# Mixer A of a hybrid encoder: the second pair of heads takes its chunks in exchanged order, and the low-rank operand is padded to 128 rows

## The chip, the cores and the metric

The kernel is one program on one core of a Trainium2 chip. Its engines are TensorE (PE; its weight loads are listed as PEld), VectorE (DVE), ScalarE (ACT), GpSimd (POOL) and SyncE (SP), which issues DMAs. Each engine works through its own queue in order and waits on semaphores for the others. The metric is the device time of one execution in microseconds (us), less is better; a kernel's time is the median of its runs.

## What is computed

A two-layer encoder over 1024 tokens of width 1024. In each layer the normed input goes through one input product into four mixers A, B, C and D of 256 columns each, through an output product and then through a feed-forward network. Mixer A is the one that is changed: a recurrence over tokens with a 64x64 state per head, four heads.

```python
def _rwkv7_scan(r, w, k, v, kk, b):
    def step(state, inp):
        r_t, w_t, k_t, v_t, kk_t, b_t = inp
        sa = jnp.einsum('bhvk,bhk->bhv', state, -kk_t)
        state = (state * w_t[:, :, None, :]
                 + sa[..., None] * b_t[:, :, None, :]
                 + v_t[..., None] * k_t[:, :, None, :])
        return state, jnp.einsum('bhvk,bhk->bhv', state, r_t)
...
def _rwkv7_mixer(p, mu, w0, w_up, a0, a_up, g_up, k_k, k_a, r_k, ln_g, ln_b):
    p = p + (p_prev - p) * mu
    r, k, v, wd, ad, gd = _split(p, A_SIZES)
    w_log = -jax.nn.softplus(-(w0 + jnp.tanh(wd) @ w_up).astype(f32)) - 0.5
    decay = jnp.exp(-jnp.exp(w_log))
    a = jax.nn.sigmoid((a0 + ad @ a_up).astype(f32))
    g = jax.nn.sigmoid(gd) @ g_up
```

`w_up` and `a_up` have 32 rows, `g_up` has 64: these are the low-rank products.

## The kernel before

The sequence is worked through in two halves of 512 tokens per layer. The large products (input, output and feed-forward products) are written in `product`, `product2` and `pair`: they run on PE with 128 rows and 128 columns of the array, 512 or 256 moving columns, and their results stand in the PSUM tile `pm`. Here they are called the main products. Beside them run the mixers as generators that are stepped by `weave` and `beside`; a scheduler of the language then sets one fixed order per engine from priorities and its own cost model, so that mixer instructions stand between main products in PE's queue.

Mixer A (`mixA`, `piece`) goes over a half in four blocks of 128 tokens, so there are 16 pieces in all. A block is two chunks of 64 tokens (`par` 0 and 1), and its four heads are two pairs (`hp` 0 and 1) of two (`h`). All its products stand in the PSUM tile `pa`, a bank of 128x512. A piece runs these groups of products; PE runs a product in f32 as two records in the trace:

- the low-rank products with the weights `lw`: two single ones for the decay, two for `a`, on 32 rows of the array, and two for the gate on 64 rows; in the trace `pa<-lora,cst`;
- `pa<-RA,KB`: the products of keys and queries inside a chunk pair, eight of 64 rows; their masked results are the tiles `G`;
- the inverse of a triangular matrix per chunk and head in `solve` (VectorE) and `inverse`: a first level of 16x16 blocks (`pa<-DT,G` and `pa<-D,V`, 16 products each on tiles of 32x32) and a second of 32x32 blocks (`pa<-XT,G` and `pa<-D,VT`, four products each per chunk);
- for each chunk, one after the other since the state `M` goes from one into the next: `part` (`pa<-cst,RA` and `pa<-VS,G`, six products, 12 records, whose result lies on 64 partitions, so on half of the array's columns), then a copy to `Us`, then `pa<-Us,Xs` (four products of 64x64), a copy into `VS`, a second `part` for the output `Y`, and `pa<-VS,KBt`, which with the whole array updates the state;
- transposes and the product with `rkH` with the whole array.

In `part` both pairs of heads work on the same chunk, so that all its products of one call use the same 64 columns of the array.

Of the kernel before, what the change touches and what calls it, by code (L numbers as in the profile page):

```python
# [85 lines left out]
class Kern:  # L86
# [133 lines left out]
    def consts(self):  # L220
# [45 lines left out]
        self.plast = self.const([128, L, UA], "plast")  # L266
        self.M = [self.const([128, 128], f"M{hp}") for hp in range(2)]
# [26 lines left out]
    def layer_params(self, l):  # L294
# [5 lines left out]
        self.lw = self.const([128, 256], "lw")  # L300
        nc.sync.dma_start(out=self.lw, in_=a["lora"][l])
# [416 lines left out]
    def shifted(self, l, hf, b, u, n, name):  # L718
# [14 lines left out]
        for i in range(n):  # L733
            self.act(o[:, i, :], t[:, i, 1:], AF.Copy, scale=self.omu[:, u + i:u + i + 1])
            self.stt(o[:, i, :], t[:, i, 0:128], self.pc[l]["mu"][:, u + i:u + i + 1], o[:, i, :], ALU.mult, ALU.add)
        return o

    def piece(self, l, hf, b, lo):
# [9 lines left out]

        Lc = self.sa([128, 2, 128], name="Lc")
        ta = self.sa([128, 2, 128], name="ta")  # L750
        ps = self.misca()
        for hp, cc, ch in hps:
            self.mm(ps[:, ch], self.lw[0:32, ch], lo[0:32, :], True, True, (0, 0))
            self.act(Lc[:, hp, :], ps[:, ch], AF.Tanh, scale=0.5, bias=self.hw0[:, cc])
        ps = self.misca()
        for hp, cc, ch in hps:
            self.mm(ps[:, ch], self.lw[32:64, ch], lo[32:64, :], True, True, (32, 0))
            self.act(ta[:, hp, :], ps[:, ch], AF.Tanh, scale=0.5, bias=self.ha0[:, cc])
# [88 lines left out]

        Y = self.sa([128, 2, 128], name="Y")
        for par in range(2):
            u0, y0 = 64 * (1 - par), 64 * par  # L850
            us, ys = slice(u0, u0 + 64), slice(y0, y0 + 64)
            heads = [(hp, h, slice(64 * h, 64 * h + 64), slice(hp * 128 + h * 64, hp * 128 + h * 64 + 64))
                     for hp in range(2) for h in range(2)]
# [17 lines left out]
            nc.scalar.copy(out=Y[ys], in_=ps[ys, 0:256].rearrange("p (r d) -> p r d", r=2))  # L871
            for hp, cc, ch in hps:
                self.mm(ps[:, 256 + hp * 128:384 + hp * 128], KBt[:, hp * 2 + par, :], VS[:, hp, par, :], True, True)
            mt = self.sa([128, 2, 128], name="mt")
            for hp, cc, ch in hps:
                self.tt(mt[:, hp, :], ps[:, 256 + hp * 128:384 + hp * 128], self.M[hp], ALU.add)
                self.stt(self.M[hp], mt[:, hp, :], WC[:, hp * 2 + par:hp * 2 + par + 1], self.cs["mH"], ALU.mult, ALU.mult)
# [17 lines left out]
        for hp, cc, ch in hps:  # L895
            nc.tensor.transpose(ps[:, ch], Y[:, hp, :], self.ident)
            self.act(yt[:, hp, :], ps[:, ch], AF.Identity, scale=c["rlng"][:, cc], bias=c["rlnb"][:, cc])
        self.tt(yt, yt, v, ALU.add)
        ps = self.misca()
        for hp, cc, ch in hps:  # L900
            self.mm(ps[:, ch], self.lw[64:128, ch], lo[64:128, :], True, True, (64, 0))
# [44 lines left out]
    def inverse(self, G, XB):  # L946
# [24 lines left out]
        for par, o, e in blocks:  # L971
            for ix in range(4):
# [11 lines left out]
        for par in range(2):  # L984
            p0 = 64 * (1 - par)
            a, b = slice(p0, p0 + 32), slice(p0 + 32, p0 + 64)
            for ix in range(4):
                self.mm(ps[b, ix * 32:ix * 32 + 32], G[par][a, ix, p0 + 32:p0 + 64], XT[a, ix * 32:ix * 32 + 32], True, True, (p0, p0 + 32))
            nc.scalar.copy(out=VT[b].rearrange("p i t -> p (i t)"), in_=ps[b, 0:128])
            for ix in range(4):  # L990
                self.mm(ps[a, 128 + ix * 32:160 + ix * 32], VT[b, ix, :], D[b, ix, :], True, True, (p0 + 32, p0))
            nc.scalar.copy(out=Xs[a, :, 32:64], in_=ps[a, 128:256].rearrange("p (i t) -> p i t", i=4))
# [340 lines left out]
NCOL = 6728  # L1333
# [17 lines left out]
WC = 16  # L1351
# [191 lines left out]
```

## Time and profile before

| | us |
|---|---|
| median of 3 runs (lowest, highest) | 3074.94 (3074.18, 3076.03) |
| the profiled execution | 3089.47 |
| its span, first to last instruction | 3087.7 |
| PE busy | 2959.4 |
| PE's weight loads busy | 2487.4 |
| DVE busy | 2068.9 |
| ACT busy | 1372.4 |
| POOL busy | 620.8 |

A row of a timeline gives the start in us from the span's start, the time from the first start to the last end of a run of like instructions, engine, line, operation, output and inputs, the part of the array (rows\*columns), the shape of the input, and the count. Matmuls are pipelined: the next one starts before the end of the one ahead, so what a product costs is read from starts rather than from durations. The granted clock is TensorE's as a share of its full 2.4 GHz.

### The profile page before, as it was taken

The page shows a single profiled execution, that of the slowest core. Times are in us where ns is not written, and L with a number is a line of the kernel's source. Part 1 is how long each engine was busy: PE and PEld are TensorE (multiplying, and loading weights), DVE is VectorE, ACT ScalarE, POOL GpSimd, SP SyncE. Part 2 cuts the span into 40 slices and gives each one's busy share as a digit, 9 for nine tenths or more (in the row PEclk, how much of TensorE's full clock was granted, in tenths as well). Part 3 has the DMA queues.
Part 4 walks back from the last instruction along what each step waited for, and adds up shares of the span by engine and source line. Part 5 has one row for each costly group of instructions (what it writes and reads, how often), then busy time and mean ns, then how long its engine had stood idle before and what let it go on. Part 6 is the DMA issues. An engine that isn't in the chain of part 4 may idle for free.

```text
span 3087.7 us, 49210 instructions
## 1 busy us (share of the span) xinstructions
PE 2959.4 (96%) x17560; PEld 2487.4 (81%) x17560; DVE 2068.9 (67%) x4721; ACT 1372.4 (44%) x2732; POOL 620.8 (20%) x659
## 2 busy tenths in 40 slices
PE   6999998999989999999999999998999999999999
PEld 5887886877778888987888887987778888878887
DVE  4667676689697675668774656567677665555555
ACT  3445443344354444454544433455454445333333
POOL 2016253246451010100111111110111111111111
PEclk8999987889999999999999999999999999999999
DMA  7458555445452424463423224553333332513332
GB/s 258 137 162 276 160 176 155 134 143 166 150 170 74 124 89 147 144 194 97 133 87 111 82 90 152 147 165 115 96 90 104 104 111 65 204 59 101 113 97 75
DMA packets 276596, 405.74 MB, mean 131 GB/s; under 512 B 74496, under 2 KB 148736, under 8 KB 276352
## 3 DMA queue, kind: packets, MB, share of 16 engines
q1 hardware_dynamic: 276352, 402.61, 41.7%
q8 instruction: 139, 2.28, 0.3%
q14 instruction: 105, 0.86, 0.1%
HBM read 343.47 MB, written 59.02 MB: 130 GB/s over the span
## 4 chain that ended last, share of the span: by engine, by line
PE 52%; DVE 2%; ACT 1%; DMA 1%; issue 1%; SPq 1%; POOL 0%; ACTq 0%; DVEq 0%; POOLq 0%
PE pm L186 44%; PE pa L186 3%; PE px L186 2%; PE S L186 1%; PE px L1088 1%; PE pn L186 0%; DMA raw<-pA 0%; ACT hr L494 0%; DVE hr L189 0%; DMA wr<-in_wout 0%; ACT L198 0%; PE px L1030 0%; DMA wr<-in_wint 0%; DMA NB<-G 0%; SPq L915 0%
## 5 line engine op out<-in xcount | busy, mean ns | idle before, releaser
L186 PE MATMUL pm<-hh,hr 128*128 128x512 f32 (+1 forms) x3328 | 1095.9, 403 | 24.4 <-ACT p L198 13.5
L186 PEld LDWEIGHTS pm<-hh,hr 128*128 128x128 f32 (+1 forms) x3328 | 627.4, 190 | 168.5 <-issue 10.9
L494 ACT CAST hr<-wr 128x1024 fp32r<-128x1024 f32 (+2 forms) x496 | 426.6, 862 | 638.5 <-PE pm L186 531.4
L189 DVE TENSOR_TENSOR hr<-wr,hr 128x1024 fp32r<-128x1024 f32 (+2 forms) x496 | 511.6, 1033 | 270.2 <-ACT hr L494 261.6
L186 PE MATMUL pm<-hl,hr 128*128 128x512 f32 (+1 forms) x1664 | 667.7, 401 | 3.1 <-DVE hl L195 3.1
L186 PE MATMUL pm<-mh,hr 128*128 128x512 f32 x1408 | 462.6, 399 | 5.4 <-ACT Lc L198 2.1
L186 PE MATMUL pm<-hr,hh 128*128 128x256 f32 x2048 | 399.9, 293 | 0.0
L186 PEld LDWEIGHTS pm<-hl,hr 128*128 128x128 f32 (+1 forms) x1664 | 316.6, 190 | 71.3 <-DVE hl L195 5.3
L186 PEld LDWEIGHTS pm<-hr,hh 128*128 128x128 f32 x2048 | 327.3, 195 | 7.2 <-issue 0.5
L660 POOL TENSOR_TENSOR y<-y,y 128x512 f32<-128x512 f32 x88 | 117.4, 1334 | 1050.7 <-DVE y L189 376.9
L186 PEld LDWEIGHTS pm<-mh,hr 128*128 128x128 f32 x1408 | 265.8, 189 | 62.0 <-ACT Lc L198 2.3
L195 DVE SCALAR_TENSOR_TENSOR y<-pm,cst,y 128x511 f32<-128x511 f32 x352 | 261.7, 744 | 73.2 <-ACT y L198 69.2
L186 PE MATMUL pm<-hr,hl 128*128 128x256 f32 x1024 | 295.6, 290 | 0.0
L186 PE MATMUL pm<-ml,hr 128*128 128x512 f32 x704 | 276.9, 393 | 0.0
L195 DVE SCALAR_TENSOR_TENSOR x<-pm,cst,x 128x512 f32<-128x512 f32 x224 | 167.1, 747 | 140.2 <-PE pm L186 139.7
L198 ACT ACTIVATE p<-S,cst 128x512 f32<-128x512 f32 (+3 forms) x288 | 165.5, 581 | 104.6 <-DVE cst L189 69.1
L186 PEld LDWEIGHTS pm<-hr,hl 128*128 128x128 f32 x1024 | 199.0, 195 | 1.6 <-issue 0.2
L1066 DVE TENSOR_REDUCE cst<-S 128x1 f32<-128x512 f32 (+3 forms) x288 | 154.0, 549 | 61.4 <-PE S L186 59.8
L186 PEld LDWEIGHTS px<-V,ct 128*128 128x128 f32 x1152 | 154.2, 200 | 30.2 <-ACT ct L1090 21.6
L186 PE MATMUL px<-V,ct 128*128 128x64 f32 x1152 | 157.9, 280 | 17.3 <-ACT ct L1090 15.4
L186 PE MATMUL pm<-yh,hr 128*128 128x512 f32 x512 | 166.1, 398 | 6.6 <-ACT yh L618 5.8
L198 ACT ACTIVATE y<-pm,cst 128x512 f32<-128x512 f32 x176 | 136.9, 778 | 76.4 <-PE pm L186 75.9
(237 smaller groups left out, 4130.6 us busy)
## 6 DMA issues: line engine op xcount, KB each, us to landing
wr<-in_up SPq DMA_DIRECT2D x176, 512.0 KB
ar<-in_ada SPq DMA_DIRECT2D x192, 256.0 KB
wr<-in_wint SPq DMA_DIRECT2D x64, 512.0 KB
wr<-in_down SPq DMA_DIRECT2D x128, 256.0 KB
wr<-in_wout SPq DMA_DIRECT2D x32, 512.0 KB
wr<-in_win SPq DMA_DIRECT2D x28, 512.0 KB
ks<-qkB SPq DMA_DIRECT2D x192, 64.0 KB
wr<-in_down SPq DMA_DIRECT2D x64, 192.0 KB
```

The source lines that it names most:

```text
L186: return self.nc.tensor.matmul(out, lhsT, rhs, start=start, stop=stop, **kw)
L189: self.nc.vector.tensor_tensor(out=out, in0=a, in1=b, op=op)
L195: self.nc.vector.scalar_tensor_tensor(out=out, in0=a, scalar=s, in1=b, op0=op0, op1=op1)
L198: self.nc.scalar.activation(out=out, in_=in_, func=func, **k)
L494: self.nc.scalar.copy(out=h, in_=r)
L660: nc.gpsimd.tensor_tensor(out=ya, in0=ya, in1=yg, op=ALU.mult)
L1066: nc.vector.tensor_reduce(out=nm[:, i:i + 1], in_=S_[:, 0:n], axis=AX.X, op=ALU.max, negate=True)
L1088: nc.tensor.transpose(ps[:, j:j + 128], pc[:, j:j + 128], self.ident)
```

## The change

In every step the second pair of heads (`hp` 1) now takes the other place of the two chunks in its tiles. This is done by exchanging the two groups of 64 tokens of that pair where its operands are read (`swapped`, in `shifted`, in the low-rank products and at the end of `piece`). Step `step` treats chunk `step` of both pairs, but its rows lie on `par = (step, 1 - step)`: on different halves of the 128 partitions, and so of the array's columns.

- `part`, the `Us` products and both levels of `inverse` are written so that products on different tiles of the array alternate; the second level takes both halves in one loop, where it had one loop after the other.
- `Us` and `Y` are copied as 128x128 where they were 64x256. `VS` is copied in two parts, by VectorE and by ScalarE, where VectorE copied both.
- `pa<-RA,KB` is written as 16 products of 64x64 in place of eight of 64x128.
- The low-rank weights are laid out as three matrices of 128 rows, zero outside their own rows, so that the products take all 128 rows of the operand.

```diff
-        self.lw = self.const([128, 256], "lw")
-        nc.sync.dma_start(out=self.lw, in_=a["lora"][l])
+
+        for i, r in enumerate((slice(0, 32), slice(32, 64), slice(64, 128))):
+            nc.sync.dma_start(out=self.lw[r, i, :], in_=a["lora"][l, r, :])
...
+            if i:
+                oi = oi.rearrange("p (c t) -> p c t", c=2)
+                t1, t0_ = self.swapped(t1), self.swapped(t0_)
...
+    def swapped(self, t):
+
+        return t.rearrange("p (c t) -> p c t", c=2)[:, ::-1, :]
...
-            self.mm(ps[:, ch], self.lw[0:32, ch], lo[0:32, :], True, True, (0, 0))
+            self.mm(ps[:, ch], self.lw[:, 0, ch], los[hp], True, True)
...
-                for h in range(2):
-                    hs = slice(64 * h, 64 * h + 64)
-                    self.mm(pss[h][:, i * 128:i * 128 + 128], flat(KB[hs, hp, 2 * par:2 * par + 2, :]),
-                            flat(RA[hs, hp, 2 * par:2 * par + 2, :]), True, True, (64 * h, 0))
+                for cq in range(2):
+                    for h in range(2):
+                        hs = slice(64 * h, 64 * h + 64)
+                        self.mm(pss[h][64 * cq:64 * cq + 64, i * 128:i * 128 + 128], KB[hs, hp, 2 * par + cq, :],
+                                flat(RA[hs, hp, 2 * par:2 * par + 2, :]), True, True, (64 * h, 64 * cq))
...
-            def part(rows, r0, j):
-
-                for hp, cc, ch in hps:
-                    self.mm(ps[rows, ch], RA[:, hp, 2 * par + j, :], self.M[hp], True, False, (0, r0))
-                    for p, h, hs, o in heads:
-                        if p == hp:
-                            self.mm(ps[rows, o], G[par][:, hp * 2 + h, rows], VS[:, hp, par, hs], False, h == 1, (0, r0))
-
-            part(us, u0, 1 - par)
-            Us = self.sa([128, 256], name="Us")
-            nc.scalar.copy(out=Us[us, :], in_=ps[us, 0:256])
-            for hp, h, hs, o in heads:
-                self.mm(ps[us, 256 + o.start:256 + o.stop], Xs[us, hp * 2 + h, :], Us[us, o], True, True, (u0, u0))
-            nc.vector.tensor_copy(VS[us, :, par, :], ps[us, 256:512].rearrange("p (r d) -> p r d", r=2))
-            part(ys, y0, par)
+            def part(rows, r0, c0, j):
+
+                for hp in range(2):
+                    s = par[hp]
+                    self.mm(ps[rows[hp], c0:c0 + 128], RA[:, hp, 2 * s + (1 - s if j else s), :], self.M[hp], True, False, (0, r0[hp]))
+                for h in range(2):
+                    for hp in range(2):
+                        self.mm(ps[rows[hp], c0 + 64 * h:c0 + 64 * h + 64], G[par[hp]][:, hp * 2 + h, rows[hp]],
+                                VS[:, hp, par[hp], 64 * h:64 * h + 64], False, h == 1, (0, r0[hp]))
+
+            part(us, u0, 0, 1)
+            Us = self.sa([128, 128], name="Us")
+            nc.scalar.copy(out=Us, in_=ps[:, 0:128])
+            for h in range(2):
+                for hp in range(2):
+                    self.mm(ps[us[hp], 128 + 64 * h:192 + 64 * h], Xs[us[hp], hp * 2 + h, :], Us[us[hp], 64 * h:64 * h + 64],
+                            True, True, (u0[hp], u0[hp]))
+            nc.vector.tensor_copy(VS[us[0], 0, par[0], :], ps[us[0], 128:256])
+            nc.scalar.copy(out=VS[us[1], 1, par[1], :], in_=ps[us[1], 128:256])
+            part(ys, y0, 256, 0)
...
-        for par, o, e in blocks:
-            for ix in range(4):
+        for ix in range(4):
+            for par, o, e in blocks:
                 self.mm(ps[o:o + 32, ix * 32:ix * 32 + 16], G[par][o:o + 16, ix, o:o + 32], DT[o:o + 16, ix * 32:ix * 32 + 16], True, True, (o, o))
...
-            for ix in range(4):
+        for ix in range(4):
+            for par, p0, a, b in halves:
                 self.mm(ps[b, ix * 32:ix * 32 + 32], G[par][a, ix, p0 + 32:p0 + 64], XT[a, ix * 32:ix * 32 + 32], True, True, (p0, p0 + 32))
```

The scheduler makes a new order for every engine. Three places show what becomes of it. The first is PE at the first call of `part` in the first piece, in the kernel before. `G_2097` is the tile of chunk 0, `VS` and `RA` are operands, `cst` holds the state, `pm` is a main product.

```order
L186 MATMUL pm<-hr,hh 128x256 x2
L186 MATMUL pm<-hr,hl 128x256
L186 MATMUL pa<-cst,RA 64x128
L186 MATMUL pa<-VS,G_2097 64x64 x2
L186 MATMUL pa<-cst,RA 64x128
L186 MATMUL pa<-VS,G_2097 64x64 x2
L186 MATMUL pm<-hr,hh 128x256 x2
```

The same call in the changed kernel, where `G_2100` and `G_2101` are the tiles of chunk places 0 and 1:

```order
L186 MATMUL pm<-hr,hh 128x256
L186 MATMUL pa<-cst,RA 64x128 x2
L186 MATMUL pa<-VS,G_2100 64x64
L186 MATMUL pa<-VS,G_2101 64x64
L186 MATMUL pa<-VS,G_2100 64x64
L186 MATMUL pa<-VS,G_2101 64x64
L186 MATMUL px<-V,ct 128x64
```

The products of one pair stood behind those of the other; now one of each pair follows one of the other.

The second place is PE at the inverse's second level, chunk place 1 of the same piece, in the kernel before (chunk place 0 stands in an earlier burst of its own, with `G_2097`):

```order
L186 MATMUL pm<-hr,hl 128x256
L186 MATMUL pm<-hr,hh 128x256
L186 MATMUL pa<-XT,G_2098 32x32 x4
L186 MATMUL pm<-hr,hh 128x256
L186 MATMUL pm<-hr,hl 128x256
```

and in the changed kernel:

```order
L186 MATMUL pm<-hr,hl 128x256
L186 MATMUL pm<-hr,hh 128x256 x2
L186 MATMUL pa<-XT,G_2100 32x32
L186 MATMUL pa<-XT,G_2101 32x32
L186 MATMUL pa<-XT,G_2100 32x32
L186 MATMUL pa<-XT,G_2101 32x32
L186 MATMUL pa<-XT,G_2100 32x32
L186 MATMUL pa<-XT,G_2101 32x32
L186 MATMUL pa<-XT,G_2100 32x32
L186 MATMUL pa<-XT,G_2101 32x32
L186 MATMUL pm<-hr,hl 128x256
```

Two bursts between main products became one of eight products that alternate.

The third place is ACT at the first state step. In the kernel before the copy of `Us` is followed by other stages' work and then by the copy of `Y`:

```order
L866 COPY Us<-pa 64x256
L546 COPY pt<-pm 128x512
L494 CAST hr<-wr 128x1024
L1090 COPY ct<-px 128x128
L198 ACTIVATE v<-raw,cst 128x128 x2
L198 ACTIVATE yB<-px,cst 128x64
L198 ACTIVATE p,cst<-S,cst 128x256 x2
L871 COPY Y<-pa 64x256
```

In the changed kernel a copy of half of `VS` stands between them, behind other stages' instructions:

```order
L884 COPY Us<-pa 128x128
L198 ACTIVATE yB<-px,cst 128x64
L198 ACTIVATE p,cst<-S,cst 128x256 x2
L549 COPY pt<-pm 128x512
L497 CAST hr<-wr 128x1024
L198 ACTIVATE v<-raw,cst 128x128
L890 COPY VS<-pa 64x128
L198 ACTIVATE v<-raw,cst 128x128
L1117 COPY ct<-px 128x256
L198 ACTIVATE p,cst<-S,cst 128x384 x2
L892 COPY Y<-pa 128x128
```

The second `part` of the step waits for this copy and for VectorE's.

## Rows read from the trace of the kernel before

**Rows 1.** The page's first part: busy time, share of the span, instructions of each engine.

```profile
PE 2959.4 (96%) x17560; PEld 2487.4 (81%) x17560; DVE 2068.9 (67%) x4721; ACT 1372.4 (44%) x2732; POOL 620.8 (20%) x659
```

**Rows 2.** Sums by stretch, PE: stretch, length, busy (records), granted clock, DMA share, GB/s.

```profile
440.00:830.00 390.00, 355.38 (x1988) 0.85 0.50 154
830.00:2650.00 1820.00, 1776.24 (x10592) 0.98 0.38 117
```

**Rows 3.** The same sums for PE's work on mixer A's tile pa alone.

```profile
80.00:440.00 360.00, 60.54 (x658) 0.98 0.58 182
440.00:830.00 390.00, 57.57 (x573) 0.85 0.50 154
830.00:2650.00 1820.00, 195.61 (x2162) 0.98 0.38 117
```

**Rows 4.** Timeline of PE around one call of part.

```profile
205.79 0.40 PE L186 MATMUL pm<-hr,hh 128*128 128x256 f32 x2
206.03 0.28 PE L186 MATMUL pm<-hr,hl 128*128 128x256 f32 x1
206.24 0.43 PE L186 MATMUL pa<-cst,RA 128*64 128x128 f32 x2
206.51 0.40 PE L186 MATMUL pa<-VS,G 128*64 128x64 f32 x4
206.74 0.38 PE L186 MATMUL pa<-cst,RA 128*64 128x128 f32 x2
206.96 0.39 PE L186 MATMUL pa<-VS,G 128*64 128x64 f32 x4
207.28 0.50 PE L186 MATMUL pm<-hr,hh 128*128 128x256 f32 x2
```

**Rows 5.** Timeline of PE around the state update, which has the whole array.

```profile
238.11 0.39 PE L186 MATMUL pm<-hl,hr 128*128 128x512 f32 x1
238.33 0.39 PE L186 MATMUL pm<-hh,hr 128*128 128x512 f32 x1
238.56 0.61 PE L186 MATMUL pa<-VS,KBt 128*128 128x128 f32 x4
238.93 0.48 PE L186 MATMUL pm<-hh,hr 128*128 128x512 f32 x1
```

**Rows 6.** Timeline of PE around one low-rank product.

```profile
106.03 0.28 PE L186 MATMUL pm<-hr,hl 128*128 128x256 f32 x1
106.24 0.48 PE L186 MATMUL pa<-lora,cst 32*128 32x128 f32 x2
106.65 0.50 PE L186 MATMUL pm<-hr,hh 128*128 128x256 f32 x2
```

**Rows 7.** Timeline of PE around one burst of RA-KB.

```profile
199.99 0.28 PE L186 MATMUL pm<-hr,hl 128*128 128x256 f32 x1
200.20 1.16 PE L186 MATMUL pa<-RA,KB 64*128 64x128 f32 x8
201.28 0.50 PE L186 MATMUL pm<-hr,hh 128*128 128x256 f32 x2
```

**Rows 8.** Timeline of PE: products of the modulation, on four column strips in turn.

```profile
31.56 3.64 PE L186 MATMUL pm<-ar,cst 128*32 128x128 f32 x64
```

**Rows 9.** Timeline of PE: one burst of the Us products.

```profile
210.80 0.68 PE L186 MATMUL pa<-Us,Xs 64*64 64x64 f32 x8
```

**Rows 10.** Timeline of PE around one burst of the inverse's second level.

```profile
187.82 0.28 PE L186 MATMUL pm<-hr,hh 128*128 128x256 f32 x1
188.03 0.43 PE L186 MATMUL pa<-XT,G 32*32 32x32 f32 x8
188.39 0.38 PE L186 MATMUL pm<-hr,hh 128*128 128x256 f32 x1
```

**Rows 11.** Timeline of PE: one burst of the inverse's first level.

```profile
170.00 0.88 PE L186 MATMUL pa<-DT,G 16*32 16x16 f32 x32
```

**Rows 12.** Waits of PE: who waited for whom, total us, times, longest.

```profile
PE pa L186 <- DVE VS L869: 2.7, 2, 2.1
```

More of the change, by code (lines that the diff above doesn't have):

```diff
@@ L266, in consts @@
         self.plast = self.const([128, L, UA], "plast")
+        self.lw = self.const([128, 3, 256], "lw")
+        nc.gpsimd.memset(self.lw, 0.0)
         self.M = [self.const([128, 128], f"M{hp}") for hp in range(2)]
@@ L747, in flat @@
             return t.rearrange("p a b -> p (a b)")
+        los = (lo, self.swapped(lo))
         Lc = self.sa([128, 2, 128], name="Lc")
@@ new lines, in piece @@
+        for step in range(2):
+            par = (step, 1 - step)
+            u0 = [64 * (1 - s) for s in par]
+            us = [slice(u, u + 64) for u in u0]
+            y0 = [64 * s for s in par]
+            ys = [slice(y, y + 64) for y in y0]
+            ps = self.misca()
+            def part(rows, r0, c0, j):
[16 more added lines that the diff above has]
+            part(ys, y0, 256, 0)
+            nc.scalar.copy(out=Y[:, step, :], in_=ps[:, 256:384])
@@ L872, in piece @@
             for hp, cc, ch in hps:
-                self.mm(ps[:, 256 + hp * 128:384 + hp * 128], KBt[:, hp * 2 + par, :], VS[:, hp, par, :], True, True)
+                self.mm(ps[:, ch], KBt[:, hp * 2 + par[hp], :], VS[:, hp, par[hp], :], True, True)
             mt = self.sa([128, 2, 128], name="mt")
             for hp, cc, ch in hps:
-                self.tt(mt[:, hp, :], ps[:, 256 + hp * 128:384 + hp * 128], self.M[hp], ALU.add)
-                self.stt(self.M[hp], mt[:, hp, :], WC[:, hp * 2 + par:hp * 2 + par + 1], self.cs["mH"], ALU.mult, ALU.mult)
+                self.tt(mt[:, hp, :], ps[:, ch], self.M[hp], ALU.add)
@@ L878, in piece @@
+                self.stt(self.M[hp], mt[:, hp, :], WC[:, hp * 2 + par[hp]:hp * 2 + par[hp] + 1], self.cs["mH"], ALU.mult, ALU.mult)
             yield
@@ L896, in piece @@
             nc.tensor.transpose(ps[:, ch], Y[:, hp, :], self.ident)
-            self.act(yt[:, hp, :], ps[:, ch], AF.Identity, scale=c["rlng"][:, cc], bias=c["rlnb"][:, cc])
-        self.tt(yt, yt, v, ALU.add)
+        p4 = ps[:, 0:256].rearrange("p (a t) -> p a t", a=4)
+        for hp, cc, ch in hps:
+            self.act(four(yt)[:, hp], p4[:, 1:3, :] if hp else p4[:, 0:4:3, :], AF.Identity, scale=c["rlng"][:, cc], bias=c["rlnb"][:, cc])
+        self.tt(yt[:, 0, :], yt[:, 0, :], v[:, 0, :], ALU.add)
+        self.tt(four(yt)[:, 1], four(yt)[:, 1], self.swapped(v[:, 1, :]), ALU.add)
         ps = self.misca()
         for hp, cc, ch in hps:
-            self.mm(ps[:, ch], self.lw[64:128, ch], lo[64:128, :], True, True, (64, 0))
+            self.mm(ps[:, ch], self.lw[:, 2, ch], lo, True, True)
         self.tt(flat(yt), flat(yt), ps[:, 0:256], ALU.mult)
@@ L966, in inverse @@
         blocks = [(par, 64 * (1 - par) + 32 * e, e) for par in range(2) for e in range(2)]
-        for par, o, e in blocks:
-            for ix in range(4):
+        for ix in range(4):
+            for par, o, e in blocks:
                 self.mm(ps[o:o + 32, ix * 32:ix * 32 + 16], G[par][o:o + 16, ix, o:o + 32], DT[o:o + 16, ix * 32:ix * 32 + 16], True, True, (o, o))
         nc.scalar.copy(out=V[:, :, 0:16], in_=ps[:, 0:128].rearrange("p (i t) -> p i t", i=4)[:, :, 0:16])
-        for par, o, e in blocks:
-            for ix in range(4):
+        for ix in range(4):
+            for par, o, e in blocks:
                 self.mm(ps[o:o + 32, 128 + ix * 16:144 + ix * 16], V[o:o + 32, ix, :], D[o:o + 32, ix, 16:32], True, True, (o, o))
@@ L983, in inverse @@
         ps = self.misca()
[L984 to L987, printed above, removed]
+        halves = [(par, 64 * (1 - par), slice(64 * (1 - par), 64 * (1 - par) + 32), slice(64 * (1 - par) + 32, 64 * (1 - par) + 64))
+                  for par in range(2)]
+        for ix in range(4):
+            for par, p0, a, b in halves:
                 self.mm(ps[b, ix * 32:ix * 32 + 32], G[par][a, ix, p0 + 32:p0 + 64], XT[a, ix * 32:ix * 32 + 32], True, True, (p0, p0 + 32))
+        for par, p0, a, b in halves:
             nc.scalar.copy(out=VT[b].rearrange("p i t -> p (i t)"), in_=ps[b, 0:128])
-            for ix in range(4):
+        for ix in range(4):
+            for par, p0, a, b in halves:
                 self.mm(ps[a, 128 + ix * 32:160 + ix * 32], VT[b, ix, :], D[b, ix, :], True, True, (p0 + 32, p0))
+        for par, p0, a, b in halves:
             nc.scalar.copy(out=Xs[a, :, 32:64], in_=ps[a, 128:256].rearrange("p (i t) -> p i t", i=4))
@@ L1332 @@
 PN, PO = 6000, 1
-NCOL = 6728
+NCOL = 7240
 PX = 5500
```

14 lines of the change are left out of this document (5 added, 9 removed).

## The prediction

> **What bounds the kernel now.** I read the busy shares first: PE is busy 96% of the span [rows 1], so the question is whether that holds where mixer A runs, and what a product of mixer A costs PE. The sums by stretch come next [rows 2]: from 830 to 2650 us PE is busy 1776 of 1820 us at a granted clock of 0.98, and from 440 to 830 us it is busy 355 of 390 at 0.85. So in the long stretch there is little for PE to wait for, and time taken off PE's queue is time off the span; in the short one the clock has been lowered for a part of it and the gaps are larger, so less of a saving arrives. The same sums for mixer A's tile alone [rows 3] tell how its work lies: 60.5 + 195.6 = 256.1 of its 313.7 us (82%) lie in 80 to 440 and 830 to 2650 us, and 57.6 us (18%) in the short stretch. From 2650 us on there is none.
>
> Busy time is not what a burst costs. **How a burst is priced:** between main products PE starts one every 0.12 us (205.79 to 206.03 for two, 256 columns, [rows 4]) or 0.22 us (238.11 to 238.33, 512 columns, [rows 5]). I take the start of the main product behind a burst minus the start of the last one ahead, less one such step, and add what the pair behind lasts longer than usual (in [rows 4] 0.50 instead of 0.40 us for two of 256, in [rows 5] 0.48 instead of 0.39 for one of 512), since the second of the pair starts late.
>
> **The change part by part.** There are 16 pieces (two layers, two halves, four blocks of 128 tokens). A program product in f32 shows as two records.
>
> *The low-rank products* (four single ones per piece for decay and a, one pair for the gate) had 32 or 64 rows of the array, and have all 128 now, padded with zeros. Before, a single one costs 106.65 - 106.03 - 0.12 + 0.10 = 0.60 us [rows 6]. What the same shape costs with the whole array is the KBt burst of four records: 238.93 - 238.33 - 0.22 + 0.09 = 0.47 us, so 0.12 a record and 0.24 for two [rows 5]. The difference is what PE loses in going into and out of a tiled shape: 0.60 - 0.24 = 0.36 us, 64 times, 23.0 us. The gate's pair is four records on 64 rows; the nearest row is the RA-KB burst of eight on 64 rows, 201.28 - 199.99 - 0.12 + 0.10 = 1.27 us [rows 7]; less four records of 0.12 that is 0.79, against 0.47 after, 0.32 us, 16 times, 5.1 us. Together **28.1 us**. The decay's product now waits for all rows of the low-rank operand, a tanh and an affine step more; I take nothing, and as a bound the nearest wait of PE for a VectorE result in this mixer, 1.35 us on the mean [rows 12], at 16 pieces: 22 us.
>
> *The state products* (`part`, 64 bursts). One costs 207.28 - 206.03 - 0.12 + 0.10 = 1.23 us [rows 4]. All twelve records of one lie on the same 64 columns; the six of one pair take 206.96 - 206.51 = 0.45 us. Now the pairs lie on different column halves and alternate. Do halves run side by side? The trace has the answer for column strips: 64 records of 128 columns in a row, each on the next of four strips, take 3.64 us, 0.057 each [rows 8], half or less of the 0.12 of [rows 5]. So the second pair's 0.45 us is hidden behind the first: 64 x 0.45 = **28.8 us**.
>
> *The Us products* (32 bursts of eight records). They alternate now between two diagonal quarters. Eight take 0.68 us [rows 9], the last four of VS-G in [rows 4] 0.39, so four fewer in line are worth 0.29: 32 x 0.29 = **9.3 us**, if quarters overlap.
>
> *The inverse's second level.* Two bursts of eight records became one of sixteen on two tiles, for XT-G and for D-VT alike. One burst costs 188.39 - 187.82 - 0.12 + (0.38 - 0.28) = 0.55 us [rows 10]. With the tiles side by side, sixteen cost what eight do: a burst is saved, 2 x 16 x 0.55 = **17.6 us**. If they ran in line, eight more records would take at most 188.39 - 188.03 = 0.36 us, and 0.19 would be left: 6.1 us, the lower end.
>
> *The inverse's first level.* 32 records on four diagonal tiles take 0.88 us one tile after the other [rows 11]; cycled, each tile has eight, as in [rows 10], 0.43. Saved 0.45 us, for DT-G and for D-V, which has as many: 2 x 16 x 0.45 = **14.4 us**. Lower end nothing.
>
> First the rows on that: in [rows 11] 32 records take 0.88 us where eight on one tile take 0.43, so a further one costs (0.88 - 0.43)/24 = 0.019 us, less than half of 0.36/8 = 0.045 in line; tiles of different rows and columns overlap already where one follows another, though all write one bank. The Trainium skill ("TensorEngine Tiling (Array Packing)", Restrictions and Gotchas, Gotcha 1) says that different row tiles cannot access the same PSUM bank simultaneously. By that rule the two inverse levels and Us would keep their order in line, and the result would be the second rival's; the trace speaks against it.
>
> *RA-KB.* Eight records of 64 rows and 128 columns became sixteen of 64 by 64, alternating halves. Side by side they take the same time: I take zero. In line they would add 8 x (201.28 - 200.20)/8 = 1.08 us to each of 32 bursts, 34.6 us.
>
> *Pieces.* In the new order of PE some bursts are cut by other products that stand in between, RA-KB above all: I count some 15 more fragments than before. Going in and out costs about 0.2 to 0.3 us (0.60 - 0.24 above, less): **minus 4 us**.
>
> *Other engines.* Us and Y are copied as 128x128 rather than 64x256, which is less ACT time. The second half of VS, one copy on DVE, is one on DVE and one on ACT. PE waits for DVE's copy twice in the whole run, 2.7 us in all, 2.1 the longest [rows 12]. Behind it in PE's queue stands `part`, and behind that the main products, all held while it waits. On ACT the copy may queue behind another stage's work. Lower bound zero, upper bound the mean of those two waits at each of 32 steps, 32 x 1.35 = 43 us; I take zero, since ACT's Us copy in the same chain has no entry among PE's waits of that size. One more memset and four more parameter loads are outside every chain: zero.
>
> **Sum.** 28.1 + 28.8 + 9.3 + 17.6 + 14.4 - 4 = 94.2 us of PE's queue. 82% of it, 77 us, comes off in full; of the 17 us in the short stretch I take half, 8.5. That is 86 us: a span of 3087.7 - 86 = 3002. The profiled execution itself took 3089.47 us, 14.5 above the median of the plain runs, 3074.94; I take the saving off the median: **2989 us**.
>
> **The rivals.**
> *Rival 1, the gain returns as waits.* PE's queue shortens, but the chain of a piece (copies on ACT and DVE, two trips through DRAM) doesn't, and the ACT copy of VS is late at most steps. Against: 44 us of idle in 1820. Price: the 43 us above; 3075 - 86 + 43 = 3032.
> *Rival 2, tiles of different rows don't run together.* Then Us gives nothing (-9.3), the second level 6.1 instead of 17.6, the first nothing (-14.4): 94.2 - 35.2 = 59 us, of which 91% (86 of 94) arrive, 54: 3021. Against it, [rows 11]. For it stands the Trainium skill's sentence above.
> *Rival 3, no tiles run together.* Left are 28.1 + 6.1 - 34.6 = about zero: 3075, no change; the alternation does not do what it says. Against: [rows 8].
> *Rival 4, slower.* Each change of tile empties the array, as the entry into a tiled shape does now: 206.24 - 206.03 - 0.12 = 0.09 us. The new orders alternate some 78 times more per piece (20 in `part`, 6 in Us, 14 in the second level, 24 in the first, 14 in RA-KB): 1248 x 0.09 = 112 us on top of rival 3: 3187. With no overlap it decides from 5 ns per alternation. Against: 64 alternations at 0.057 us with the product included.
> *Rival 5, more.* The short stretch gains in full too, and shorter bursts of small products there let the clock stay up: another 17 us and more; 2968.
>
> **How the numbers follow.** Forecast 0.60 (about 2972 to 3010), rival 1 0.17, rival 2 0.07, rival 3 0.04, rival 4 or another slowdown 0.06, rival 5 0.06. The range runs from rival 5 to beyond rival 1: 2963 to 3038, leaving out rivals 3 and 4 and the tails. A measurement of this kernel tells 0.2% (6 us) from no change. Faster is everything but rivals 3 and 4: 0.90; same 0.04; slower 0.06.
>
> **What would show it.** Right: single low-rank products at 0.24 us with no longer main product behind; `part` at about 0.78 us; sixteen XT-G records within about 0.45; RA-KB still about 1.25. Wrong: alternating records spaced as before (rival 3) or wider (rival 4); PE's waits for VS on ACT over 20 us (rival 1).

## The result and the profile after

The changed kernel takes 3024.1 us, median of 4 runs (3017.75 to 3029.51), beside 3075.49 for the kernel before (4 runs). The ratio is 0.9831, with an interval of 0.9816 to 0.9846: 47 to 57 us less, 51 at the median. The forecast was 2989 with a range of 2963 to 3038, so the sign and the range held, and the saving was 51 us where 86 had been expected. The time lies outside the band of 2972 to 3010 that the prediction gave its main case, and close to the 3032 of its rival 1.

The profiled execution took 3017.75 us. The page's first part, which answers to [rows 1]:

```profile
PE 2871.6 (95%) x17816; PEld 2419.6 (80%) x17816; DVE 2073.8 (69%) x4737; ACT 1361.4 (45%) x2760; POOL 609.2 (20%) x660
```

PE's busy time fell by 87.8 us. Its idle time rose: 3087.7 - 2959.4 = 128.3 us before, 3016.0 - 2871.6 = 144.4 us after. So PE was relieved of about as much as forecast, and a part of that came back as idle time. (The two profiled executions lie 14 us above and 6 us below the medians of their kernels, so what is read from them can be off by that much.)

The bursts, from PE's timeline after (start, us, engine, line, operation, array, shape, count). In order: a low-rank product, RA-KB, the inverse's second level, Us, `part`, the inverse's first level.

```profile
99.53 0.40 PE L186 MATMUL pm<-hr,hh 128*128 128x256 f32 x2
99.78 0.38 PE L186 MATMUL pa<-lora,cst 128*128 128x128 f32 x2
99.91 0.36 PE L186 MATMUL pm<-hr,hl 128*128 128x256 f32 x1
...
115.59 0.28 PE L186 MATMUL pm<-hr,hh 128*128 128x256 f32 x1
115.80 1.09 PE L186 MATMUL pa<-RA,KB 64*64 64x128 f32 x16
116.82 0.39 PE L186 MATMUL pm<-hr,hh 128*128 128x256 f32 x1
...
172.63 0.40 PE L186 MATMUL pm<-hr,hh 128*128 128x256 f32 x2
172.96 0.44 PE L186 MATMUL pa<-XT,G 32*32 32x32 f32 x16
173.33 0.38 PE L186 MATMUL pm<-hr,hl 128*128 128x256 f32 x1
...
196.01 0.28 PE L186 MATMUL pm<-hr,hl 128*128 128x256 f32 x1
196.22 0.45 PE L186 MATMUL pa<-Us,Xs 64*64 64x64 f32 x8
196.60 0.39 PE L186 MATMUL pm<-hr,hh 128*128 128x256 f32 x1
...
200.96 0.28 PE L186 MATMUL pm<-hr,hl 128*128 128x256 f32 x1
201.17 0.44 PE L186 MATMUL pa<-cst,RA 128*64 128x128 f32 x4
201.44 0.40 PE L186 MATMUL pa<-VS,G 128*64 128x64 f32 x8
201.77 0.50 PE L186 MATMUL pm<-hr,hh 128*128 128x256 f32 x2
...
1265.55 0.28 PE L186 MATMUL pm<-hr,hl 128*128 128x256 f32 x1
1265.76 0.44 PE L186 MATMUL pa<-DT,G 16*32 16x16 f32 x32
1266.13 0.51 PE L186 MATMUL pm<-hr,hh 128*128 128x256 f32 x2
```

Priced by the prediction's rule (the last main product ahead of a burst is the second of a x2 row, so 0.12 us after that row's start):

| burst | before | forecast | after |
|---|---|---|---|
| one low-rank product | 0.60 [rows 6] | 0.24 | 99.91 - 99.65 - 0.12 + 0.08 = 0.22 |
| `part` | 1.23 [rows 4] | 0.78 | 201.77 - 200.96 - 0.12 + 0.10 = 0.79 |
| second level, XT-G | two of 0.55 [rows 10] | one of 0.55 | 173.33 - 172.75 - 0.12 + 0.10 = 0.56 |
| first level, DT-G, first start to last end | 0.88 [rows 11] | 0.43 | 0.44 |
| Us, first start to last end | 0.68 [rows 9] | 0.39 | 0.45 |
| RA-KB | 1.27 [rows 7] | 1.27 | 116.82 - 115.59 - 0.12 + 0.11 = 1.22 |

Every burst shown costs within 0.06 us of its forecast. That tiles work at the same time shows in the records one by one: the first two of `pa<-cst,RA`, on the two column halves, start 7 ns apart, where 512 columns of a main product take 0.22 us, so that their 128 columns would take some 55 ns (an estimate from [rows 5]). What has to be explained above all is what the end of the kernel makes of this.

**Where the time went.** To compare stretches in which the same work is done, I cut each execution where 35% of its 11272 main-product records have started; this is the *mark*, and it lies near 1100 us. Sums by stretch on both sides of it (stretch, length, busy time and records of PE, PEld, DVE, ACT, POOL, granted clock, DMA share, GB/s), before and then after:

```profile
0.00:1136.00 1136.00, 1052.61 (x6741) 894.86 (x6742) 823.95 (x2034) 507.54 (x1087) 367.67 (x422) 0.92 0.51 159
1136.00:3083.00 1947.00, 1906.05 (x10818) 1592.29 (x10817) 1244.17 (x2686) 864.81 (x1645) 253.12 (x237) 0.98 0.37 115
```

```profile
0.00:1108.00 1108.00, 1009.62 (x6949) 859.09 (x6950) 833.59 (x2041) 500.14 (x1098) 362.84 (x427) 0.93 0.52 163
1108.00:3012.00 1904.00, 1861.65 (x10868) 1560.52 (x10867) 1239.42 (x2696) 861.23 (x1663) 246.32 (x233) 0.98 0.38 118
```

Behind the mark, PE idles 41 us before and 42 us after; its busy time falls by 44 and the stretch by 43. Up to the mark, busy time falls by 43 and the stretch by 28 only, since idle time rises from 83 to 98 us.

Busy time also holds what a lowered clock costs. The records give the granted clock from moment to moment, so I take half of PE's busy time at the lower level (1.2 GHz, where the upper is 2.4) as lost, which is an estimate, and call the rest *work*. Each stretch is then work + idle + clock loss:

| us | up to the mark: length = work + idle + clock | behind it: length = work + idle + clock |
|---|---|---|
| before | 1136 = 980 + 83 + 72 | 1947 = 1877 + 41 + 29 |
| after | 1108 = 947 + 98 + 63 | 1904 = 1829 + 42 + 33 |
| padding alone | 1122 = 971 + 94 + 57 | 1940 = 1863 + 48 + 29 |
| inverse alone | 1128 = 970 + 96 + 62 | 1954 = 1864 + 55 + 34 |
| exchange alone | 1108 = 967 + 77 + 64 | 1937 = 1864 + 47 + 26 |
| before, other order | 1103 = 981 + 76 + 47 | 1963 = 1880 + 48 + 35 |
| after, other order | 1089 = 951 + 93 + 46 | 1901 = 1828 + 47 + 26 |
| no alternation | 1095 = 961 + 76 + 59 | 1920 = 1847 + 46 + 27 |
| more PE work early | 1138 = 1009 + 90 + 39 | 1895 = 1827 + 44 + 23 |
| more PE work late | 1105 = 947 + 96 + 61 | 1988 = 1884 + 65 + 40 |

(All but the first two are experiments below. Lengths and terms are rounded one by one.) In all, work fell by 82.5 us, from 2858.3 to 2775.8, where the sum of the prediction was 94.2.

What holds up the end in the two stretches shows in the chain that ended last, here for 440 to 900 us and for 1400 to 1950 us of the kernel after:

```profile
by line: PE pm L186 26.1%; issue 6.8%; DMA ar<-in_ada 6.4%; DVE hr L189 4.7%; PE pa L186 3.9%; PE px L186 3.7%; DVE cst L195 3.1%; DVE y L195 2.5%; DVE av L403 2.2%; DVE cst L1093 2.0%; DVE cst L189 2.0%; DVE p L195 1.9%; PE S L186 1.6%; SP
...
by line: PE pm L186 77.6%; PE pa L186 5.4%; PE px L186 2.5%; PE S L186 1.9%; DMA raw<-pA 1.3%; PE px L1115 1.2%; DMA XB<-cst 1.0%; SPq L980 1.0%; DMA wr<-in_win 0.9%; issue 0.9%; PE pn L186 0.7%; DVE cst L189 0.6%; DVE ht L195 0.5%; DVE hl 
```

In the late stretch over three quarters of the chain are main products and 5.4% are mixer A's own; in the early one only 26% are main products, and the rest is spread over DVE, DMA and ACT. Between 440 and 830 us DVE is busy for 329 of 390 us after the change (the line gives PE, PEld, DVE, ACT and POOL as above):

```profile
440.00:830.00 390.00, 352.96 (x2049) 291.51 (x2045) 328.80 (x692) 161.37 (x350) 197.74 (x135) 0.89 0.52 163
```

The waits of PE up to the mark (who waited for whom, total us, times, longest), some lines of before:

```profile
PE pm L186 <- DMA ar<-in_ada: 11.1, 4, 9.1
PE px L186 <- ACT ct L1090: 7.7, 8, 2.8
PE pa L186 <- DVE VS L869: 2.7, 2, 2.1
```

and of after, with the wait that rival 1 named as the last:

```profile
PE px L186 <- ACT ct L1117: 12.4, 7, 4.6
PE pm L186 <- DMA ar<-in_ada: 11.0, 4, 9.0
PE pm L186 <- DVE hr L189: 6.8, 5, 3.4
PE pa L186 <- DVE cst L195: 4.0, 4, 1.8
PE pa L186 <- ACT Y L892: 3.1, 3, 2.4
PE pa L186 <- DVE lora L192: 2.7, 1, 2.7
PE pa L186 <- ACT VS L890: 0.7, 1, 0.7
```

The wait for the modulation's loads (`ar`) is the same before and after. What comes back is spread over many waits, and not only those of other stages: summed over all its waits up to the mark, PE waits 24 us ahead of mixer A's own products (`pa`) where it waited 15 before. In the second order shown below it is the other way round: 10 us ahead of `pa` where it was 20, and 32 ahead of products into `px`, which belong to other mixers, where it was 11. So which waits take the gain back depends on the order. The new ScalarE copy of `VS` costs 0.7 us in the whole run, 2.7 in the second order.

### The profile page after: what moved, and what is told of

Read it like the earlier page. It is cut to its first block, busy times and chain, and to the rows that moved or that the text cites. A ratio compares the mean times of both kernels' runs of the same rounds, so it can differ in the third digit from the quotient of the medians.

```text
span 3016.0 us, 49828 instructions
## 1 busy us (share of the span) xinstructions
PE 2871.6 (95%) x17816; PEld 2419.6 (80%) x17816; DVE 2073.8 (69%) x4737; ACT 1361.4 (45%) x2760; POOL 609.2 (20%) x660
## 4 chain that ended last, share of the span: by engine, by line
PE 75%; DVE 9%; DMA 7%; ACT 3%; issue 2%; SPq 2%; POOL 1%; DVEq 0%; ACTq 0%; POOLq 0%
PE pm L186 60%; PE pa L186 4%; PE px L186 4%; PE S L186 2%; PE px L1115 2%; DMA ar<-in_ada 2%; DVE hr L189 1%; DMA raw<-pA 1%; PE pn L186 1%; DVE cst L195 1%; DVE cst L189 1%; ACT hr L497 1%; SPq L980 1%; DMA qkB<-qh 1%; DVE cst L1093 1%
```

## The experiments

Two questions were open: whether each part of the change does to PE's work what its price says, and why a part of it doesn't reach the end.

**One part alone.** In the first kernel only the low-rank operand is padded.

```diff
-            self.mm(ps[:, ch], self.lw[0:32, ch], lo[0:32, :], True, True, (0, 0))
+            self.mm(ps[:, ch], self.lw[:, 0, ch], lo, True, True)
```

> The kernel before with the low-rank operand padded to 128 rows, and nothing else. Theory: the 64 single products fall from 0.60 us to about 0.23 each and the 16 gate pairs from 0.84 to 0.46, 28 to 30 us less in PE's queue, of which nine tenths arrive as the prediction had it: 25 us off, about 3050. Rival, waits: only the share arrives that arrived in the whole change (51 of 94): 15 us, 3060. Rival, order: the scheduler's new order moves the time by 10 us or more by itself, so the result is off both.

Measured: 3074.74 us (12 runs, 3067.43 to 3083.99), ratio 0.9995 [0.9982, 1.0009]. PE's work fell by 25 us, from 2858.3 to 2833.4, near the 28 forecast, and a single product costs 0.22 us. None of it arrived as time that can be told from the spread of the runs, which only the rival of the order allows.

In the second kernel only the inverse's loops alternate.

```diff
-        for par, o, e in blocks:
-            for ix in range(4):
+        for ix in range(4):
+            for par, o, e in blocks:
```

> The kernel before with the inverse's loops of the changed kernel (tiles alternate, both halves in one loop), and nothing else. Theory: first-level bursts fall from 1.00 to 0.56 us, 32 second-level bursts go; 32 us less in PE's queue, nine tenths arrive: 29 us off, 3046. Rival, waits: 17 us, 3058. Rival, tiles of different rows don't run together: first-level bursts stay at 1.00 us, 6 us off, 3069.

Measured: 3091.0 us (6 runs), ratio 1.0052 [1.0034, 1.0071]: slower by 15 us, although PE's work fell by 23 us (to 2834.9) where 32 had been priced. None of the three expectations had it.

In the third, only the exchange of chunks is made (`part`, `Us`, `VS` and `Y` as in the kernel after; padding, inverse and RA-KB as before).

```diff
-        for ix in range(4):
-            for par, o, e in blocks:
+        for par, o, e in blocks:
+            for ix in range(4):
...
-            self.mm(ps[:, ch], self.lw[:, 0, ch], los[hp], True, True)
+            self.mm(ps[:, ch], self.lw[0:32, ch], los[hp][0:32], True, True, (0, 0))
```

> The changed kernel with the low-rank products, RA-KB and the inverse as before: the exchange of chunks alone, with alternating part and Us products and VS copied by two engines. Theory: part falls from 1.23 to 0.79 us and Us from 0.80 to 0.57, 28 + 7 = 35 us less in PE's queue, nine tenths arrive: 32 us off, 3043. Rival, waits: 19 us, 3056, with PE's wait for VS on ACT over 10 us in sum. Rival, order: off both by 10 us or more.

Measured: 3050.08 us (5 runs), ratio 0.9912 [0.9895, 0.9929], 27 us faster; PE's work fell by 27 us (to 2830.9) where 35 had been expected, and `part` costs 0.79 us. The rival's wait for `VS` on ACT, over 10 us, isn't there: it is 0.7 us.

So the parts nearly add up in PE's work, 25 + 23 + 27 = 75 of 82.5, but not in time: none, 15 slower, 27 faster, and together 51 faster. A fixed worth of each part is refuted. Nor does a part's saving arrive wherever PE is busiest: behind the mark each part alone takes 13 to 14 us off PE's work, and the stretch becomes 7 us shorter with the padding, 10 with the exchange, and 7 longer with the inverse, where PE idles 14 us more than before:

```profile
1128.00:3082.00 1954.00, 1898.77 (x10817) 1582.77 (x10818) 1245.90 (x2692) 865.25 (x1649) 255.60 (x237) 0.98 0.37 115
```

In the fourth, the changed kernel has the RA-KB products of before.

```diff
-                for cq in range(2):
-                    for h in range(2):
-                        hs = slice(64 * h, 64 * h + 64)
-                        self.mm(pss[h][64 * cq:64 * cq + 64, i * 128:i * 128 + 128], KB[hs, hp, 2 * par + cq, :],
-                                flat(RA[hs, hp, 2 * par:2 * par + 2, :]), True, True, (64 * h, 64 * cq))
+                for h in range(2):
+                    hs = slice(64 * h, 64 * h + 64)
+                    self.mm(pss[h][:, i * 128:i * 128 + 128], flat(KB[hs, hp, 2 * par:2 * par + 2, :]),
+                            flat(RA[hs, hp, 2 * par:2 * par + 2, :]), True, True, (64 * h, 0))
```

> The changed kernel with RA-KB as before, eight products of 64x128 instead of sixteen of 64x64. Theory: 1.27 instead of 1.21 us per burst, 32 bursts, 2 us more than the changed kernel: 3026, not to be told from it. Rival, order: the built order differs in many places, and if that alone moves the time, this differs from 3024 by more than 10 us in either direction.

Measured: 3017.67 us (5 runs), ratio 0.9808 [0.979, 0.9827], about 6 us less than the kernel after. The two intervals overlap, so the 6 us are not clear of noise, and neither expectation (2 us more; over 10 us off) is borne out. Its profile isn't read.

**The same instructions in another order.** Each edit makes the scheduler build a new order for all engines. To see what that alone is worth, a constant that sets how many steps the mixers take beside the main products is changed from 90 to 92 in four kernels; no product changes.

```diff
-STEPS_A, STEPS_B = 80, 90
+STEPS_A, STEPS_B = 80, 92
```

> The kernel before with one scheduling constant changed (STEPS_B, the weight with which two generators are interleaved, 90 to 92): the same instructions, in another order from the middle of the second half's mixers on. Order theory: the losses of PE (waits and lowered clock) of a build are its order's, and vary by 10 to 20 us between builds of the same work; this one differs from the 3076 us of before by 8 us or more. Queue theory: an order this near costs the same; within 6 us.

> The changed kernel with the same constant changed, 90 to 92: the same instructions in another order. Order theory: off the 3024 us of the changed kernel by 8 us or more, in either direction. Queue theory: within 6 us.

> The kernel before with the padding alone, and the constant changed, 90 to 92. Its PE work at full clock was 25 us less than before's, and its time was the same (3074.7). Order theory: that was its order; with another one the mean of the two builds lies between 3050 and 3068. Queue theory (waits take the gain back whatever the order): 3075 again, within 6 us.

> The kernel before with the inverse's loops alone, and the constant changed, 90 to 92. PE's work was 23 us less and the time 15 us more (3091). Order theory: another order brings another loss, and 3091 was at the unlucky end, so 3080 or less. Rival, the merged loops themselves bring waits (a longer chain in a piece): 3085 to 3097 again.

| | 90 | 92 | difference |
|---|---|---|---|
| before | 3075.5 | 3071.84, ratio 0.9988 [0.9975, 1.0001] | -4 |
| padding alone | 3074.74 | 3065.36, ratio 0.9974 [0.996, 0.9988] | -9 |
| inverse alone | 3091.0 | 3067.68, ratio 0.9972 [0.9958, 0.9986] | -23 |
| after | 3024.1 | 3009.21, ratio 0.9784 [0.9761, 0.9808] | -15 |

The order alone moves a kernel by up to 23 us. The 4 us of the kernel before are not clear of noise, and less than the 8 its expectation asked for; the mean of the two padded kernels, 3070, lies outside the 3050 to 3068 expected; the other two came out as the order theory had it. All four became faster with 92, so a part of this may belong to the constant, which lets the mixers go ahead a little faster, rather than to chance; two orders don't tell. In the second order the inverse alone is 4 us faster than its own before (not clear of noise) where it was 15 slower in the first, so the slowdown is no fixed price of the alternation. In both orders padding and inverse bring far less (-1 and +15, -6 and -4 us) than the 22 to 25 us that they take off PE's work, and the whole change brings 51 and 63 of 82. Behind the mark, the second order gives padding 21 us for 15 us less work and the inverse 24 for 23, where the first gave 7 for 14 and minus 7 for 13. So what a part brings there, too, depends on the order. Sums by stretch for the pair in the second order, before:

```profile
0.00:1103.00 1103.00, 1027.41 (x6738) 873.35 (x6739) 816.89 (x2029) 504.45 (x1083) 359.46 (x422) 0.95 0.52 163
1103.00:3066.00 1963.00, 1914.57 (x10824) 1598.52 (x10822) 1246.45 (x2692) 863.76 (x1645) 251.90 (x237) 0.98 0.37 115
```

and after:

```profile
0.00:1089.00 1089.00, 996.48 (x7005) 848.90 (x7006) 829.36 (x2050) 500.82 (x1108) 364.15 (x427) 0.95 0.53 167
1089.00:2990.00 1901.00, 1853.51 (x10812) 1550.90 (x10810) 1238.43 (x2688) 852.53 (x1649) 257.11 (x233) 0.98 0.38 118
```

It is the same picture: behind the mark 61 us less busy time and 62 us less length, up to it 31 us less busy time and 14 us less length, with idle time up from 76 to 93 us.

**The same PE work added early or late.** If PE's queue sets the pace only behind the mark, work added to it must cost much there and little ahead of it. In the kernel after, the state update's products are written nine times over in one layer (each overwrites the same result, so nothing that is computed changes).

```diff
-                self.mm(ps[:, ch], KBt[:, hp * 2 + par[hp], :], VS[:, hp, par[hp], :], True, True)
+                for _ in range(9 if l == 0 else 1):
+                    self.mm(ps[:, ch], KBt[:, hp * 2 + par[hp], :], VS[:, hp, par[hp], :], True, True)
```

> The changed kernel with the state update's products written nine times instead of once in layer 0 (the result is the same): 256 more f32 products of 0.235 us, 60 us more in PE's queue, all in the eight pieces of layer 0. Theory (until about 1100 us PE's own queue is only part of what bounds, later it is all): about half arrives, 20 to 42 us, 3045 to 3066. Rival, the return is everywhere the same: as much as in the late variant, within 10 us.

> The same 60 us of PE work in the eight pieces of layer 1. Theory: PE is the bound there and all of it arrives, 52 to 68 us, 3076 to 3092. Rival, the return is the same everywhere: about 35 us, 3060, as the early one.

Measured: in the first layer 3038.17 us (4 runs), ratio 0.9879 [0.9861, 0.9897], 14 us more than the kernel after, for 61 us more work; in the second layer (`l == 1`) 3100.62 us (5 runs), ratio 1.0085 [1.0068, 1.0102], 76.5 us more, for 56 us more work. The early kernel lies below the range expected (3045 to 3066), the late one above (3076 to 3092): the contrast is greater than the theory had it. Sums by stretch, early:

```profile
0.00:1138.00 1138.00, 1048.43 (x7491) 901.73 (x7492) 839.57 (x2063) 509.50 (x1126) 367.75 (x427) 0.95 0.52 159
1138.00:3033.00 1895.00, 1850.82 (x10838) 1549.75 (x10837) 1230.90 (x2673) 849.18 (x1631) 251.53 (x233) 0.98 0.39 118
```

and late:

```profile
0.00:1105.00 1105.00, 1008.60 (x6964) 857.28 (x6964) 831.90 (x2042) 500.78 (x1099) 361.15 (x427) 0.94 0.52 163
1105.00:3093.00 1988.00, 1923.28 (x11366) 1623.67 (x11364) 1248.12 (x2694) 859.68 (x1661) 248.89 (x233) 0.98 0.37 113
```

Early, the stretch up to the mark became 30 us longer for 62 us more work: 9 us less idle time and 24 us less lost to the lowered clock make up the rest. The clock shows most between 440 and 830 us, 0.94 here for 0.89 in the kernel after:

```profile
440.00:830.00 390.00, 357.29 (x2381) 300.76 (x2380) 322.88 (x705) 168.23 (x374) 189.70 (x150) 0.94 0.54 165
```

Behind the mark, where nothing was added, the stretch became 9 us shorter. Late, the stretch behind the mark became 84 us longer, and 22 us of that is idle time. Why PE idles more isn't shown; the added products also stand in the chain of a piece and lengthen it. So a microsecond of PE work added ahead of the mark cost 0.2 us at the end (14/61) and 0.5 up to the mark (30/62), and one added behind it cost one or more. Both kernels have orders of their own, so each cost may be off by what an order moves (up to 23 us above). The contrast between them, 62 us, is far larger than that; the size of either is not exact.

**The alternation undone.** In the kernel after, all products of this mixer's `part`, `Us` and inverse are written pair after pair and tile after tile; everything else stays.

```diff
-                for h in range(2):
-                    for hp in range(2):
+                    for h in range(2):
...
-        for ix in range(4):
-            for par, o, e in blocks:
+        for par, o, e in blocks:
+            for ix in range(4):
```

> The changed kernel with the chunks exchanged but the products written pair after pair and tile after tile, not in alternation (part, Us, both levels of the inverse). Theory: a tile's products overlap the next tile's only for their last few, as in the first level before; part about 1.0 us instead of 0.79, DT-G and D-V about 1.0 instead of 0.57, XT-G of sixteen about 0.7; some 35 us more in PE's queue: 3045 to 3065. Rival, PE reorders by itself: all as in the changed kernel, 3024 within 10 us. Rival, tiles only overlap in alternation: part 1.23 us, 45 us and more, over 3065.

Measured: 3018.98 us (5 runs), ratio 0.9815 [0.9795, 0.9836], which is 5 us less than the kernel after (not clear of noise), though PE's work is 32 us more (35 expected). The time, then, is where the rival that PE reorders by itself put it, but its account of the bursts fails. PE's timeline of that kernel, one call of `part` and one burst of XT-G:

```profile
202.74 0.28 PE L186 MATMUL pm<-hr,hl 128*128 128x256 f32 x1
202.95 0.43 PE L186 MATMUL pa<-cst,RA 128*64 128x128 f32 x2
203.22 0.22 PE L186 MATMUL pa<-VS,G 128*64 128x64 f32 x1
203.22 0.32 PE L186 MATMUL pa<-cst,RA 128*64 128x128 f32 x1
203.27 0.28 PE L186 MATMUL pa<-VS,G 128*64 128x64 f32 x2
203.38 0.27 PE L186 MATMUL pa<-cst,RA 128*64 128x128 f32 x1
203.39 0.50 PE L186 MATMUL pa<-VS,G 128*64 128x64 f32 x5
203.81 0.39 PE L186 MATMUL pm<-hr,hh 128*128 128x256 f32 x1
...
174.15 0.59 PE L186 MATMUL pa<-XT,G 32*32 32x32 f32 x16
```

`part` costs 203.81 - 202.74 - 0.12 + 0.11 = 1.06 us, between 0.79 and 1.23: the records of the second pair's first product start among those of the first pair's last ones (both rows at 203.22), which no order of whole products, two records each, would give. The sixteen XT-G records take 0.59 us where alternating ones take 0.44. The Us products take 0.46 us as against 0.45, so they overlap nearly as well without alternating. On time, the table by stretch says: up to the mark 14 us more work and 23 us less idle time, so 13 us shorter; behind the mark 19 us more work and 16 us longer. So behind the mark the alternation is worth about what it takes off PE's work; ahead of it the order that came with it loses nearly as much. In this order, then, the alternation as such brought no time that can be measured: a kernel without it, but with the pairs on different halves, has the whole gain of the change.

**A version that beats both.** The fourth kernel's RA-KB and the constant 92 together:

```diff
-STEPS_A, STEPS_B = 80, 90
+STEPS_A, STEPS_B = 80, 92
```

> The changed kernel with RA-KB as before (eight products of 64x128) and the scheduling constant at 92. RA-KB as before gave 3018 with the constant at 90, the constant at 92 gave 3009 with the new RA-KB. Order theory: the two do not add; anywhere from 3000 to 3030. Rival, RA-KB's split costs 6 us by itself: 3003.

Measured: 2997.18 us (4 runs, 2992.31 to 3000.81), ratio 0.9743 [0.9723, 0.9762]: 78 us faster than before, 27 faster than the change as made, and below both expectations. With eight products the kernel is 12 us faster in this order and 6 in the other, but each of these edits also makes a new order, and differences of this size come from the order alone. So that the split costs time isn't shown. The 32 bursts of RA-KB stand in 42 and 43 pieces in PE's order where they are split into 16 products, and in 34 where they are eight (this kernel, and before), and PE's work is 5 us less than with the split in the same order.

## Why the prediction was right in sign, and where it was too high

- **What bounds the kernel.** Right for the whole change behind the mark, wrong ahead of it. The prediction counted 80 to 440 us with the stretches where PE's queue sets the end, and expected half of the saving in 440 to 830 us. It read "PE busy" as "PE late". Up to about 1100 us PE is busy for 91 to 93%, and yet 62 us more work there cost 30 us up to the mark, and 14 at the end.
- **The prices of the bursts.** Right, each within 0.06 us, and with them the statement that tiles overlap. The sum of them was too high: work fell by 82.5 us for 94.2 forecast. The largest miss among the terms is the inverse: 23 us alone, for 32.0 forecast, though its bursts cost what was forecast; why isn't shown. `part` and Us, 38.1 forecast, took 27 off as a part alone. Us was priced by first start to last end; by the rule for bursts it is 0.80 (211.40 - 210.59 - 0.12 + 0.11, the main products beside [rows 9]) to 0.58, 7 us rather than 9.3.
- **"82% of it comes off in full; of the 17 us in the short stretch I take half"** is the step that failed. By this rule, 91% of the 82.5 us, 75, should have arrived, and 51 did. Of the 82.5 us, 49 lie behind the mark (60%) and 33 ahead of it (in the other order 52 and 30). Behind the mark the stretch became 43 us shorter, the rest going mostly to the clock, and 62 in the other order. Ahead of the mark 15 to 17 us came back as idle time, and the stretch became 28 and 14 us shorter. With the 0.2 to 0.5 that the early experiment gives, the early work is worth some 6 to 17 us, and with the later part in full the sum is 56 to 67 us; 51 and 63 were measured in the two orders. That sum is for the whole change only: in the first order the parts alone, the inverse above all, brought less than it behind the mark too. What makes up the rest can't be told from the profiles, since the profiled executions of one kernel lie up to 14 us from its median.
- **The range** held in part by luck. Its upper end stands on 43 us of waits for `VS` on ScalarE, and that wait did not come; what came back came in other places.
- **Rival 1, the gain returns as waits,** came about in part, by another mechanism. It put the wait at ScalarE's copy of `VS` at 32 steps, 43 us; that wait is 0.7 us (2.7 in the other order). What returned is 15 to 17 us, ahead of the mark, over many waits. In the first order 9 us of it stand ahead of mixer A's own products, in the second none. The wait of the padded products for the low-rank operand, which the prediction put at nothing with 22 us as a bound, is 2.7 us, once.
- **Rivals 2, 3 and 4 are refuted.** First the row: 32 records on four diagonal tiles of one bank take 0.44 us where one tile after the other takes 0.88 [rows 11], so products of different row tiles ran together though they write one bank, each tile its own partitions of it. (The prediction's own argument from [rows 11] was weaker than it looks: it set records of 16 columns against records of 32 in [rows 10].) The sentence of the Trainium skill that the prediction weighed ("TensorEngine Tiling (Array Packing)", Restrictions and Gotchas, Gotcha 1) says the contrary; here the measurement decides. Row tiles that write the same partitions were not tried. RA-KB, sixteen on two halves, takes 1.22 us for 1.27, so that no price of a change of tile shows.
- **Rival 5, more.** Not seen: the clock's loss up to the mark fell by 9 us in one order and by 1 in the other, less than the idle time that came back.
- **RA-KB, zero** and **pieces, minus 4.** A burst is no dearer. Without the split the time was 6 and 12 us less, which may be the order's. No run measures the term for pieces by itself.

What stays open: what it is in an order that makes the first 1100 us shorter or longer by 19 and 33 us with the same instructions (the two pairs of orders), and why the parts alone bring so little of their work as time. The waits there are many and short, and no experiment took one away.

## What to carry to other kernels

Products on small tiles take less of PE's queue if consecutive ones lie on different rows or columns of the array, and the saving of a burst is found from starts, not from busy time. But before a saving in an engine's queue is counted as time, ask stretch by stretch whether that queue is what ends last there: adding a known amount of work to one stretch and to another tells it in two runs, if it is more than an order moves. And where a scheduler sets the order, time one part in at least two orders before judging it; here one part was 15 us slower in one and 4 us faster in the other.

## What the runs showed of the hardware that was not expected

- Tiles of different rows and of different columns, each with its own partitions of one PSUM bank, ran side by side: 32 records in 0.44 us on four diagonal tiles, 16 in 0.44 us on two. The Us records on two diagonal quarters start in pairs 7 ns apart, the next pair 58 ns later.
- PE overlaps tiles partly by itself: written pair after pair, `part` costs 1.06 us when the pairs lie on different halves, against 1.23 when they lie on the same and 0.79 when they alternate.
- More PE work went with less loss to the clock: with 62 us more up to the mark, the granted clock between 440 and 830 us was 0.94 where it had been 0.89, and 24 us less were lost to it. But the kernel before, with the same work in two orders, lost 72 and 47 us up to the mark, so the order can do as much, and which did it isn't shown.
- Single executions of one kernel spread from 3063 to 3089 us, over 26 of the kernel before.
